# First half of a down projection as seven half-size block products in place of eight, on one Trainium2 core

## The chip, the core and the metric

The kernel runs on one core of one Trainium2 chip, in one launch. The metric is the device time of that core in microseconds. A time is the median of several executions. One further execution was recorded by the hardware profiler; the profile and the trace quoted below are from it.

The engines are TensorE (PE: matmuls; its weight loads are listed as PEld), VectorE (DVE), ScalarE (ACT), GpSimd (POOL) and SyncE (SP, which here issues most DMAs). Each works through its own queue in order and waits for the others on semaphores. PE writes into PSUM, which has eight banks of 512 float32 columns by 128 partitions; ACT and DVE read it, POOL does not in this kernel.

## The reference, cut to what matters

One encoder block over 512 tokens of width 1024. After the token mixers comes the feed-forward part, the only one that the change touches:

```python
def conv_glu_ffn(h, w_up, w_conv, b_conv, w_down):
    a, u = jnp.split(h @ w_up, 2, axis=-1)          # 2 x 2816 features
    return (jax.nn.gelu(dwconv3(a, w_conv, b_conv)) * u) @ w_down
...
x = x + merged @ w_out
x = x + conv_glu_ffn(rms_norm(x, ffn_norm_g), w_ffn_up, w_ffn_conv, b_ffn_conv, w_ffn_down)
return rms_norm(x, final_norm_g)
```

`w_down` is 2816 x 1024: 22 feature tiles of 128 by 8 output tiles of 128. All is float32.

## The kernel before

**Every product is three.** A float32 operand is split into a high part (rounded by a copy into the type float32r) and a low part (the difference). `mm3` (lines 212 to 215) multiplies high by high, high by low and low by high into one PSUM region. So a weight tile of 128 x 128 against 512 tokens is three matmuls of 512 columns, on lines 213, 214 and 215.

**The weights come in blocks.** `block_list` (line 63) names them in the order of use; each is up to 1024 columns by 128 partitions (512 KB), contiguous in `wflat`. `weights(key)` (line 201) is called where PE needs a block. It first issues the DMAs of blocks up to three ahead (`emit_raw`, into three buffers `wr`) and emits the splits of blocks up to one ahead (`emit_split`): ACT copies 512 columns into `wh` (line 195), DVE subtracts into `wl` (line 196), twice a block. `wh` and `wl` have four buffers each, that is, two blocks. A raw buffer comes free when its splits are done, a split buffer when PE has done its last matmul with it.

**The feed-forward loop** (lines 1289 to 1339) runs over two halves, `hh`, of eleven feature tiles each. For each feature tile `f` it projects `ua` and `uu` (24 matmuls of 512 columns each, into a bank of the pool `mm`), and between them runs a chain over the first: DVE scales by the row norm (line 456), ACT and DVE do the three-tap convolution (458 to 460), ACT and DVE the gelu (1315 to 1318), POOL multiplies by the row norm (1319). Then DVE multiplies with the second projection (1322) and ACT and DVE split the result into `UH[j]`, `UL[j]` (219, 220).

After eleven feature tiles comes the half's down projection: for each output tile, 11 x 3 matmuls of 512 columns accumulate into one bank, and DVE adds the bank to the residual `x2[f]` (line 1329). In the second half, output tiles 0 to 4 are done so; `last_tiles` does tiles 5 to 7: tile 5 in two halves of 256 tokens, tiles 6 and 7 for the first 256 tokens with the weights stationary, and for the last two groups of 128 tokens with the activations stationary and 256 weight columns moving (`dnl` blocks).

**What sets the order.** The source gives each engine's work in program order, and the framework's scheduler then reorders it within the dependences, so that splits of weights stand between the steps of the gate chain. Buffers that rotate (`wr`, `wh`, `wl`, the seven scratch tiles `scr`, the PSUM pools `mm` and `at` of four banks each) decide how far an engine may run ahead. The large activations lie in 15 `unit` buffers of 2112 float32 columns, four tiles of 512 and a margin of 64.

Of the kernel before, what the change touches and what calls it, by code (L numbers as in the profile page):

```python
# [17 lines left out]
P = 128  # L18
S = 512
# [3 lines left out]
M = 256  # L23
DFF = 2816
FT = DFF // P
HF = FT // 2
LF = KT - 2
NU = 15
WARM = 14
# [33 lines left out]
def block_list():  # L63

    L = []
    for i in range(4):
        L.append((("mlq", i), 1024))
    for f in range(4):
        L.append((("mlk", f), 1024))
    for c in range(3):  # L70
        for h in range(8 // TMK[c]):
            L.append((("tm", c, h), TMK[c] * TMC[c]))
    for n in ("xaq", "o", "memk", "memv", "naq", "nak"):
        for f in range(4):
# [8 lines left out]
    for hh in range(2):  # L83
        for f in range(HF * hh, HF * (hh + 1)):
            L.append((("ua", f), 1024))
            L.append((("uu", f), 1024))
        for f in range(8 if hh == 0 else LF):
            if hh == 1 and f >= LF - 3:
                i = f - LF + 3
                L.append((("dnl", i), 256 * (4 if i < 2 else 3)))  # L90
            for i, n in ((0, 8), (1, 3)):
                L.append((("dn", hh, f, i), n * 128))
    return L


# [15 lines left out]
def hybrid_block(ctx, tc, xg, xT, memT, wflat, vecs, gbias, nabias, outa, outb, outc):  # L111
# [18 lines left out]
    def unit(dt=F32):  # L130
        return up.tile([P, UNIT], dt, tag="unit", name=nm("u"))
# [11 lines left out]
        return atp.tile([P, 512], F32, tag="at", name=nm("at"))  # L143


    raws, split = {}, {}
    RAW_AHEAD, SPLIT_AHEAD = 3, 1
    st = {"raw": 0, "split": 0}

    def emit_raw(i):  # L150
        key, n = BLOCKS[i]
# [17 lines left out]
    def lastw(k, m):  # L169
# [3 lines left out]
        q = slice(k % 8 * 256, k % 8 * 256 + m)  # L173
        return lw[k // 8][:, HI256:][:, q], lw[2 + k // 8][:, q]

    def emit_split(i):
        key, n = BLOCKS[i]
        r = raws.pop(i)
        c, hs = halves(i)
        split[i] = []  # L180
        for a, b in hs:
            m = (b - a) * c
            if key[0] == "dnl":
                h, l = lastw(4 * key[1] + a, m)
            else:
                h = wp.tile([P, HWT], F32R, tag="hi", name=nm("wh"), bufs=4)
                l = wp.tile([P, HWT], F32R, tag="lo", name=nm("wl"), bufs=4)
                if key[:2] == ("tm", 2):
                    h = h[:, HI256:]
            for u, v in ((0, P), (P, 2 * P), (2 * P, m)) if i == 0 and a == 0 else ((0, m),):  # L190
                src = r[:, a * c + u:a * c + v]
                if i == 0 and u == 0:
                    st["wh1"] = V.tensor_copy(h[:, u:v], src).ins
                else:
                    A.activation(h[:, u:v], src, AF.Copy)  # L195
                V.tensor_tensor(l[:, u:v], src, h[:, u:v].bitcast(F32), op=ALU.subtract)  # L196
            for k in range(a, b):
                q = slice((k - a) * c, (k - a + 1) * c)
                split[i].append((h[:, q], l[:, q]))

    def weights(key):

        i, _, n = BINDEX[key]
        while st["raw"] <= min(i + RAW_AHEAD, len(BLOCKS) - 1):
            emit_raw(st["raw"])
            st["raw"] += 1
        while st["split"] <= min(i + SPLIT_AHEAD, len(BLOCKS) - 1):
            emit_split(st["split"])
            st["split"] += 1
        return split.pop(i)  # L210
# [948 lines left out]
    def last_tiles(U, UL_):  # L1159
# [63 lines left out]
        for t in range(2, NT):  # L1223
# [62 lines left out]
            V.scalar_tensor_tensor(o[:, LF * P:D], r, col, gfin, op0=ALU.mult, op1=ALU.mult)  # L1286
            SY.dma_start(outc[:, LF * P:], o[:, LF * P:D])

    for hh in range(2):
        gu = [unit(F32R) for _ in range(6)]  # L1290
        UH = [gu[k // 4][:, (k % 4) * S:(k % 4 + 1) * S] for k in range(HF)]
        UL = [gu[3 + k // 4][:, (k % 4) * S:(k % 4 + 1) * S] for k in range(HF)]
        for j in range(HF):
            f = HF * hh + j
# [23 lines left out]
            V.scalar_tensor_tensor(c, sq, 1.0, c, op0=ALU.add, op1=ALU.mult)  # L1318
            G.tensor_tensor(c, c, rb2, op=ALU.mult)  # L1319
# [3 lines left out]
            split_act(UH[j], UL[j], c, 0.5)  # L1323
        for f in range(KT if hh == 0 else LF - 1):
            ws = weights(("dn", hh, f, 0)) + weights(("dn", hh, f, 1))
            ps = mmps()
            for k in range(HF):
                mm3(ps, ws[k][0], ws[k][1], UH[k], UL[k], k == 0, k == HF - 1)
            V.tensor_tensor(x2[f], ps, x2[f], op=ALU.add)
            if hh == 1:  # L1330
                if f == 0:
                    A.activation(acc3, x2[f], AF.Square)
                else:
                    sq = scr()
                    A.activation(sq, x2[f], AF.Square)
                    G.tensor_tensor(acc3, acc3, sq, op=ALU.add)
                A.activation(x2[f], x2[f], AF.Copy, scale=vcol("fin_g", f))
        if hh == 1:
            last_tiles(UH, UL)


def _tiles(a):
# [4 lines left out]
def _layout(inp):  # L1347
# [14 lines left out]
    for key, n in BLOCKS:  # L1362
        kind = key[0]
        if kind == "mlq":
            b = wi[:, 2 * key[1]:2 * key[1] + 2, c_q:c_q + 512]
        elif kind in ("mlk", "o", "xaq", "naq", "nak"):
            c = {"mlk": c_k, "o": c_o, "xaq": c_xq, "naq": c_nq, "nak": c_nk}[kind] + key[1] * P
            b = wi[:, :, c:c + P]
        elif kind == "tm":
            _, c, h = key  # L1370
            ks = slice(TMK[c] * h, TMK[c] * (h + 1))
            if c == 0:
                b = np.concatenate([wi[:, ks, c_g:c_g + 16], wi[:, ks, c_v:c_v + 256]], axis=2)
            elif c == 1:
                b = np.concatenate([wi[:, ks, c_v + 256:c_v + 512], wi[:, ks, c_nv:c_nv + 256]], axis=2)
            else:
                b = wi[:, ks, c_nv + 256:c_nv + 512]
        elif kind == "memk":
            b = mkv[:, :, key[1] * P:(key[1] + 1) * P]
        elif kind == "memv":  # L1380
            b = mkv[:, 2 * key[1]:2 * key[1] + 2, 512:1024]
        elif kind == "g":
            gi = (0, 2, 1)[key[1]]
            c = c_m + gi * 1024 + key[2] * P
            b = wi[:, :, c:c + P]
        elif kind == "br":
            b = br[key[1]][:, :, key[2] * 256:(key[2] + 1) * 256]
        elif kind == "out":
            b = wo[:, :, key[1] * P:(key[1] + 1) * P]
        elif kind == "ua":  # L1390
            b = wu[:, :, key[1] * P:(key[1] + 1) * P]
        elif kind == "uu":
            b = wu[:, :, DFF + key[1] * P:DFF + (key[1] + 1) * P]
        elif kind == "dnl":
            k = HF + 4 * key[1]
            b = wd[:, k:k + n // 256, LF * P:]
        else:
            _, hh, f, i = key
            b = wd[:, HF * hh + 8 * i:HF * hh + 8 * i + n // P, f * P:(f + 1) * P]
# [54 lines left out]
```

## Time and profile before

| | us |
|---|---|
| median of 3 executions | 879.65 |
| lowest, highest | 879.35, 879.66 |
| span of the profiled execution, first to last instruction | 878.1 |
| PE busy in it | 872.7 |
| POOL busy in it | 127.1 |

Only the span is known of the profiled execution; its own time was not listed beside it. The granted TensorE clock was 0.999 over the span.

How to read the rows that follow: a row of a group gives source line, engine, operation, output<-inputs, shapes, count, then busy time and the mean ns of one, then the engine's idle time before such instructions and who ended it. A row of the timeline gives the start in us from the span's start, the duration, the engine, line, operation, operands and shape, and in brackets the idle time before it. A row of the windows gives for one stretch the busy time of each engine with its count of instructions, the granted clock, the DMA engines' share and GB/s.

### The profile page before, as it was taken

How to read it: one execution, taken by the hardware profiler on the slowest of the kernel's cores; microseconds unless marked ns; L12 is line 12 of the kernel's file. 1: busy time of each engine (PE TensorE's matmuls, PEld its weight loads, DVE VectorE, ACT ScalarE, POOL GpSimd, SP SyncE). 2: the span in 40 equal slices, each digit the busy share in tenths (PEclk: the TensorE clock that was granted, in tenths of full speed). 3: DMA queues.
4: the chain of work that ended last, by engine and by line, in shares of the span. 5: the costliest groups of instructions: out<-in, count | busy, mean ns of one | idle time of the engine just before them, and what ended most of it. 6: DMA issues, size and time to landing. Idle time of an engine off the chain costs nothing.

```text
span 878.1 us, 12238 instructions
## 1 busy us (share of the span) xinstructions
PE 872.7 (99%) x4334; PEld 740.4 (84%) x4334; DVE 582.2 (66%) x1211; ACT 451.4 (51%) x953; POOL 127.1 (14%) x203
## 2 busy tenths in 40 slices
PE   9999999999999999999999999999999999999997
PEld 7898889888888888888888888888888888888897
DVE  7694686775667758898676558776633466666433
ACT  7363555754456658888544435444422344444532
POOL 0101100001072460700000002111100011111011
PEclk9999999999999999999999999999999999999999
DMA  8224643522242354533223432222233322222412
GB/s 280 99 73 140 207 135 97 192 85 90 74 137 87 107 146 131 156 110 130 97 97 109 144 107 94 99 97 96 72 103 101 109 97 97 98 97 87 141 34 96
DMA packets 39421, 99.81 MB, mean 114 GB/s; under 512 B 5688, under 2 KB 13880, under 8 KB 39360
## 3 DMA queue, kind: packets, MB, share of 16 engines
q1 hardware_dynamic: 31568, 92.32, 31.1%
q0 software_dynamic: 7360, 6.32, 3.1%
q8 instruction: 34, 0.56, 0.3%
q10 hardware_dynamic: 432, 0.39, 0.1%
q14 instruction: 27, 0.22, 0.1%
HBM read 94.80 MB, written 4.21 MB: 113 GB/s over the span
## 4 chain that ended last, share of the span: by engine, by line
PE 99%; issue 0%; ACT 0%; DVE 0%; POOLq 0%; POOL 0%; DVEq 0%
PE mm L213 29%; PE mm L215 29%; PE mm L214 29%; PE at L214 2%; PE at L213 2%; PE at L215 2%; PE at L872 1%; PE at L725 1%; PE at L853 1%; PE at L727 1%; PE at L690 1%; PE at L834 0%; PE at L835 0%; PE at L706 0%; PE at L960 0%
## 5 line engine op out<-in xcount | busy, mean ns | idle before, releaser
L213 PE MATMUL mm<-u,wh 128*128 128x512 f32 (+1 forms) x1072 | 415.6, 388 | 0.0
L215 PE MATMUL mm<-u,wl 128*128 128x512 f32 (+1 forms) x1072 | 412.2, 385 | 0.0
L214 PE MATMUL mm<-u,wh 128*128 128x512 f32 (+1 forms) x1072 | 411.8, 384 | 0.0
L195 ACT ACTIVATE wh<-wr 128x512 fp32r<-128x512 f32 (+2 forms) x298 | 184.1, 622 | 234.4 <-PE mm L214 188.1
L196 DVE TENSOR_TENSOR wl<-wr,wh 128x512 fp32r<-128x512 f32 (+3 forms) x300 | 203.1, 678 | 92.4 <-ACT wh L195 85.8
L215 PEld LDWEIGHTS mm<-u,wl 128*128 128x128 f32 x1072 | 201.5, 188 | 40.1
L214 PEld LDWEIGHTS mm<-u,wh 128*128 128x128 f32 x1072 | 201.8, 188 | 38.8
L213 PEld LDWEIGHTS mm<-u,wh 128*128 128x128 f32 x1072 | 201.8, 188 | 38.2
L1319 POOL TENSOR_TENSOR s<-s,rb 128x512 f32<-128x512 f32 x22 | 38.3, 1739 | 250.0 <-DVE s L1318 238.1
L538 POOL DMA_DIRECT2D u<-nav_d x128 | 62.2, 512 | 66.5 <-PE at L872 22.5
L219 ACT ACTIVATE u<-s 128x512 fp32r<-128x512 f32 x26 | 16.4, 630 | 57.5 <-DVE s L1322 56.1
L1322 DVE TENSOR_TENSOR s<-mm,s 128x512 f32<-128x512 f32 x22 | 15.2, 691 | 25.1 <-POOL s L1319 25.1
L458 ACT ACTIVATE s<-pad,vec 128x512 f32<-128x512 f32 x30 | 24.4, 813 | 9.5 <-DVE pad L456 9.5
L459 DVE SCALAR_TENSOR_TENSOR s<-pad,vec,s 128x512 f32<-128x512 f32 x30 | 23.6, 786 | 6.1 <-ACT s L458 6.0
L220 DVE SCALAR_TENSOR_TENSOR u<-s,u 128x512 fp32r<-128x512 f32 x26 | 18.0, 691 | 14.1 <-ACT u L219 14.0
L1318 DVE SCALAR_TENSOR_TENSOR s<-s,s 128x512 f32<-128x512 f32 x22 | 15.2, 692 | 13.4 <-ACT s L1317 13.3
L317 POOL TENSOR_TENSOR rc<-y,nhalf 128x4 f32<-128x4 f32 x1 | 1.0, 1032 | 152.9 <-DVE y L314 152.9
L460 DVE SCALAR_TENSOR_TENSOR s<-pad,vec,s 128x512 f32<-128x512 f32 x30 | 22.5, 750 | 0.7
L1317 ACT ACTIVATE s<-s 128x512 f32<-128x512 f32 x22 | 13.9, 632 | 15.1 <-DVE s L1316 15.1
L456 DVE TENSOR_TENSOR pad<-mm,rb 128x512 f32<-128x512 f32 x22 | 15.1, 691 | 7.3 <-PE mm L215 6.5
L213 PE MATMUL mm<-wh,u 128*128 128x512 f32 x48 | 18.9, 394 | 0.0
L214 PE MATMUL mm<-wl,u 128*128 128x512 f32 x48 | 18.8, 392 | 0.0
(315 smaller groups left out, 1028.4 us busy)
## 6 DMA issues: line engine op xcount, KB each, us to landing
wr<-wflat SPq DMA_DIRECT2D x141, 512.0 KB, 3.3
nab<-nabias SPq DMA_DIRECT2D x16, 256.0 KB, 2.7
u<-nav_d POOLq DMA_DIRECT2D x128, 32.0 KB, 2.6
s<-xT SPq DMA_DIRECT2D x15, 256.0 KB, 3.9
wr<-wflat SPq DMA_DIRECT2D x14, 192.0 KB, 2.3
nav_d<-nv POOLq DMA_DIRECT2D x8, 256.0 KB, 2.4
R<-rd SPq DMA_DIRECT2D x8, 256.0 KB, 3.9
wr<-wflat SPq DMA_DIRECT2D x2, 544.0 KB, 3.3
```

Of the source, the lines that this page charges most:

```text
L195: A.activation(h[:, u:v], src, AF.Copy)
L196: V.tensor_tensor(l[:, u:v], src, h[:, u:v].bitcast(F32), op=ALU.subtract)
L213: PE.matmul(ps, lh, rh, start=start, stop=False)
L214: PE.matmul(ps, lh, rl, start=False, stop=False)
L215: st["mm"] = PE.matmul(ps, ll, rh, start=False, stop=stop).ins
L219: A.activation(h, src, AF.Copy, scale=scale)
L220: V.scalar_tensor_tensor(l, src, scale, h.bitcast(F32), op0=ALU.mult, op1=ALU.subtract)
L458: A.activation(t1, pad[:, 0:512], AF.Identity, scale=vcol(w, i), bias=vcol(b, i))
L459: V.scalar_tensor_tensor(t1, pad[:, 1:513], vcol(w, n + i), t1, op0=ALU.mult, op1=ALU.add)
L460: V.scalar_tensor_tensor(t1, pad[:, 2:514], vcol(w, 2 * n + i), t1, op0=ALU.mult, op1=ALU.add)
L538: G.dma_start(vw[r * 32:(r + 1) * 32, i * 256:(i + 1) * 256], nav_v[hf, r, CW[b]:CW[b] + 32, hp * 256:(hp + 1) * 256])
L1319: G.tensor_tensor(c, c, rb2, op=ALU.mult)
```

## The change

The first half shrinks from eleven feature tiles to ten, the second grows to twelve. For the first half, two feature tiles, two output tiles and two halves of the tokens form a product of 2 x 2 blocks. The blocks are 128 x 128 of the weights and 128 x 256 of the activations. It is computed in Winograd's form of Strassen's scheme: seven products of 256 columns instead of eight, with four sums of weight blocks and four sums of activation blocks formed first, and the seven results combined afterwards. Each of the seven products is again three matmuls (`mm3`), and accumulates in PSUM over the five feature pairs.

- `emit_sum`: POOL forms the weight sums from the raw block, three additions, up to two blocks ahead. A new block kind `ds` carries two feature pairs (1024 columns) or one (512) of one output pair, three blocks for each of the four output pairs.
- `split_block`: ACT and DVE split seven weight tiles per feature pair instead of four. The sums' parts go to tiles `sh`, `sl`, with four buffers each.
- `strip`: after every second feature tile DVE forms the activation sums (four operations of 256 columns), and ACT and DVE split 7 x 256 columns instead of 4 x 256 (two tiles). The strips are placed 16 or 48 float32 past the start of a `unit`.
- `products`: 105 matmuls of 256 columns per output pair into four banks, from `at` and `mm` in turn. Then one ACT copy, three DVE operations of 256 columns and two of 512 that read PSUM, and two POOL additions of 512 close the pair.

```diff
-HF = FT // 2
+HFS = (10, 12)
+HF = HFS[1]
+NP = HFS[0] // 2
...
+    for fp in range(4):
+        for b in range((NP + 1) // 2):
+            L.append((("ds", fp, b), 512 * min(2, NP - 2 * b)))
...
-    RAW_AHEAD, SPLIT_AHEAD = 3, 1
+    RAW_AHEAD, SUM_AHEAD, SPLIT_AHEAD = 3, 2, 1
...
+    def emit_sum(i):
...
+        r, w = raws[i], n // 4
+        s31 = tp.tile([P, S], F32, tag="E", name=nm("s31"))[:, :2 * w]
+        s24 = tp.tile([P, S], F32, tag="nab", name=nm("s24"))[:, :2 * w]
+        G.tensor_tensor(s31, r[:, :2 * w], r[:, w:3 * w], op=ALU.add)
+        G.tensor_tensor(s24[:, :w], s31[:, w:], r[:, :w], op=ALU.add)
+        G.tensor_tensor(s24[:, w:], s24[:, :w], r[:, 3 * w:4 * w], op=ALU.add)
...
+    def split_block(i):
...
+        for src, names, small in ((r[:, :w], ("a11",), True), (r[:, 2 * w:4 * w], ("a22", "a12"), True),
+                                  (s31, ("s3", "s1"), False), (s24, ("s2", "s4"), False)):
...
+                h = tp.tile([P, S], F32R, tag="R", name=nm("sh"), bufs=4)[:, :m]
+                l = tp.tile([P, S], F32R, tag="H", name=nm("sl"), bufs=4)[:, :m]
+            A.activation(h, src, AF.Copy)
+            V.tensor_tensor(l, src, h.bitcast(F32), op=ALU.subtract)
...
+    def products(fp):
+
+        bank = [(mmps if fp % 2 else atps)() for _ in range(4)]
...
+        (p2, p3), (p4, p5), (p1, p6) = [halves_of(t) for t in bank[:3]]
+        p7 = bank[3][:, :S // 2]
+        plan = (("a11", p1, "b11", True, False), ("a12", p2, "b21", True, False), ("s4", p3, "b22", False, True),
+                ("a22", p4, "t4", True, False), ("s1", p5, "t1", False, True), ("s2", p6, "t2", False, True),
+                ("s3", p7, "t3", True, True))
+        for p in range(NP):
+            g = p % 2
+            if g == 0:
+                ws = weights(("ds", fp, p // 2))
+            gs = slice(g * P, (g + 1) * P)
+            for a, ps, b, first, last in plan:
+                (wh, wl), (xh, xl) = ws[a], strips[p][b]
+                mm3(ps, wh[:, gs], wl[:, gs], xh, xl, first and p == 0, last and p == NP - 1)
...
+        A.activation(z[:, :Hs], p1, AF.Copy)
+        V.tensor_tensor(u[:, :Hs], p6, z[:, :Hs], op=ALU.subtract)
+        V.scalar_tensor_tensor(z[:, Hs:], u[:, :Hs], -1.0, p5, op0=ALU.mult, op1=ALU.subtract)
+        V.tensor_tensor(u[:, Hs:], u[:, :Hs], p7, op=ALU.add)
+        V.tensor_tensor(r1, bank[0], r1, op=ALU.add)
+        V.tensor_tensor(r2, bank[1], r2, op=ALU.add)
+        G.tensor_tensor(r1, r1, z, op=ALU.add)
+        r2v = r2.rearrange("p (a b) -> p a b", a=2)
+        G.tensor_tensor(r2v, r2v, u[:, Hs:].unsqueeze(1).to_broadcast([P, 2, Hs]), op=ALU.add)
...
+    def strip(c):
...
+        b1, b2 = held.pop(), c
+        p, Hs = len(strips), S // 2
+        sh = 16 if p < 3 else 48
...
+        V.tensor_tensor(t13[:, lo], b1[:, hi], b1[:, lo], op=ALU.subtract)
+        V.tensor_tensor(t24[:, lo], b2[:, hi], t13[:, lo], op=ALU.subtract)
+        V.tensor_tensor(t13[:, hi], b1[:, hi], b2[:, hi], op=ALU.subtract)
+        V.tensor_tensor(t24[:, hi], b2[:, lo], t24[:, lo], op=ALU.subtract)
...
+        for src, names in ((b1[:, lo], ("b11",)), (b2, ("b21", "b22")), (t13, ("t1", "t3")), (t24, ("t2", "t4"))):
+            h, l = place(Hs * len(names))
+            split_act(h, l, src, 0.5)
...
-        for f in range(KT if hh == 0 else LF - 1):
+        if hh == 0:
+            for fp in range(4):
+                products(fp)
+            continue
+        for f in range(LF - 1):
```

In the changed program the addition of a pair's first bank to the residual is on line 1358, that of its second on line 1359; the closing POOL additions are on 1360 and 1362, the splits of the new blocks on 209 and 210, the weight sums on 190 to 192.

More of the change, by code (lines that the diff above doesn't have):

```diff
@@ L82, in block_list @@
         L.append((("out", f), 1024))
[L83 to L92, printed above, removed]
+    for f in range(HFS[0]):
+        L.append((("ua", f), 1024))
+        L.append((("uu", f), 1024))
+    for fp in range(4):
+        for b in range((NP + 1) // 2):
+            L.append((("ds", fp, b), 512 * min(2, NP - 2 * b)))
+    for f in range(HFS[0], FT):
+        L.append((("ua", f), 1024))
+        L.append((("uu", f), 1024))
+    for f in range(LF):
+        if f >= LF - 3:
+            L.append((("dnl", f - LF + 3), 1024))
+        for i, n in ((0, 8), (1, 4)):
+            L.append((("dn", 1, f, i), n * 128))
     return L
@@ L143, in atps @@
         return atp.tile([P, 512], F32, tag="at", name=nm("at"))
-    raws, split = {}, {}
-    RAW_AHEAD, SPLIT_AHEAD = 3, 1
-    st = {"raw": 0, "split": 0}
+    raws, split, sums = {}, {}, {}
+    RAW_AHEAD, SUM_AHEAD, SPLIT_AHEAD = 3, 2, 1
+    st = {"raw": 0, "sum": 0, "split": 0}
     def emit_raw(i):
@@ L206, in weights @@
             st["raw"] += 1
+        while st["sum"] <= min(i + SUM_AHEAD, len(BLOCKS) - 1):
+            emit_sum(st["sum"])
+            st["sum"] += 1
         while st["split"] <= min(i + SPLIT_AHEAD, len(BLOCKS) - 1):
@@ L1398, in _layout @@
             _, hh, f, i = key
-            b = wd[:, HF * hh + 8 * i:HF * hh + 8 * i + n // P, f * P:(f + 1) * P]
+            b = wd[:, HFS[0] + 8 * i:HFS[0] + 8 * i + n // P, f * P:(f + 1) * P]
         b = np.ascontiguousarray(b).reshape(P, -1)
```

86 lines of the change are left out of this document (69 added, 17 removed).

## The prediction

> **What bounds the kernel now.** I read the page's first lines first, then the chain of work that ended last, then the groups by line, then the timeline of TensorE and the windows in the feed-forward part.
>
> ```profile
> span 878.1 us, 12238 instructions
> PE 872.7 (99%) x4334; PEld 740.4 (84%) x4334; DVE 582.2 (66%) x1211; ACT 451.4 (51%) x953; POOL 127.1 (14%) x203
> ...
> PE 99%; issue 0%; ACT 0%; DVE 0%; POOLq 0%; POOL 0%; DVEq 0%
> ```
>
> TensorE (PE) is the whole chain, so the span moves by what is taken out of the row of matmuls, plus each time that row has to wait. The window inside the first down projection shows what the other engines do there now:
>
> ```profile
> core 0: us, PE busy (x) PEld busy (x) DVE busy (x) ACT busy (x) POOL busy (x), PEclk, DMA share, GB/s
> 632.00:691.80 59.80, 59.80 (x265) 49.52 (x264) 21.77 (x34) 14.95 (x25) 0.28 (x1) 1.00 0.30 99
> ```
>
> The stage runs at the full granted clock (1.00), VectorE (DVE) is busy 21.8 of 59.8 us and GpSimd (POOL) 0.3. That cover is what the change spends.
>
> A matmul's "mean ns" (384 to 388 on the page) is not its price, since the records overlap. The price is the distance from start to start:
>
> ```profile
> 799.75 0.39 PE L213 MATMUL mm<-u,wh 128*128 128x512 f32 x1
> ...
> 843.95 0.39 PE L213 MATMUL mm<-u,wh 128*128 128x512 f32 x1
> ...
> 846.67 0.28 PE L213 MATMUL mm<-u,wh 128*128 128x256 f32 x1
> ...
> 850.63 0.28 PE L213 MATMUL mm<-u,u 128*128 128x256 f32 x1
> ...
> 858.28 0.28 PE L215 MATMUL mm<-u,u 128*128 128x256 f32 x1
> ```
>
> ```profile
> 83.52 0.28 PE L213 MATMUL at<-wh,u 128*128 128x256 f32 x1
> ...
> 94.71 0.28 PE L215 MATMUL at<-wh,u 128*128 128x256 f32 x1
> ```
>
> - 512 columns: 195 steps (65 triples) in 44.20 us, 0.2267 us each.
> - 256 columns, both operands at addresses that are multiples of 256 bytes: 33 steps to 850.63 in 3.96 us, 0.1200 each.
> - 256 columns, one operand 192 bytes off such an address: 65 steps in 7.65 us, 0.1177; and 95 steps in 11.19 us, 0.1178.
>
> Half the columns thus cost 52 to 53% of a full matmul, so seven halves for eight must give 12.5% and pay back about 4%.
>
> **The change on TensorE.** The first half has now 8 output tiles x 11 feature tiles x 3 = 264 matmuls of 512 columns: 264 x 0.2267 = 59.84 us (the window above lies inside it). Afterwards: 4 output pairs x 5 feature pairs x 7 products x 3 = 420 matmuls of 256. The new strips lie 64 or 192 bytes off (`sh`), the weights on multiples of 256, so I take 0.1177: 49.43 us; the other bound, 0.1200, gives 50.40. The eleventh feature tile moves to the second half and costs there 5 x 3 full matmuls (3.40), 6 of 256 columns for the tile done in two halves (0.72), and 12 more in the last tiles (1.41): 5.53 us. Sum: 49.43 + 5.53 - 59.84 = **-4.88 us**, at 0.1200 **-3.91**. The weight load does not forbid it: loads of 0.19 us follow each other 0.12 apart while 256-column matmuls run.
>
> ```profile
> 850.51 0.19 PEld L213 LDWEIGHTS mm<-u,u 128*128 128x128 f32 x1
> 850.63 0.19 PEld L214 LDWEIGHTS mm<-u,u 128*128 128x128 f32 x1
> ```
>
> **Handovers on PSUM.** An output pair now takes four banks, alternating between the two pools. The order lists of the built program put the addition that frees the first bank (L1358 there) ahead of the rest; that bank's products p2 and p3 are finished four products before the pair ends, 12 x 0.1177 = 1.4 us, and the addition takes 0.69 us (row below). So the next up projection, which needs this bank, should not wait; if the addition came last it would cost about 2 us, once.
>
> ```profile
> L1329 DVE TENSOR_TENSOR u<-mm,u 128x512 f32<-128x512 f32 x13 | 9.0, 692 | 14.6 <-PE mm L215 14.6
> ```
>
> **What the weights now need.** An output pair takes PE 105 x 0.1177 = 12.36 us. For it come three raw blocks (two feature pairs, two, one). POOL makes sums of each (adds of 512, 256, 256 columns; 256, 128, 128 for the small one), ACT and DVE split 1792 columns instead of 1024, and each pair ends with five DVE operations that read PSUM and two POOL additions of 512. Rows:
>
> ```profile
> L195 ACT ACTIVATE wh<-wr 128x512 fp32r<-128x512 f32 x278 | 173.4, 628 | 210.3 <-PE mm L214 168.0 <-PE mm L215 10.5 <-DMA wr<-wflat 9.1
> L1177 ACT ACTIVATE s<-u 128x256 f32<-128x256 f32 x4 | 1.7, 416 | 8.1 <-DVE u L1175 8.1
> L196 DVE TENSOR_TENSOR wl<-wr,wh 128x512 fp32r<-128x512 f32 x279 | 191.4, 687 | 75.6 <-ACT wh L195 69.0 <-PE at L214 2.0 <-PE at L310 2.0
> L717 DVE TENSOR_TENSOR E<-E,u 128x256 f32<-128x256 f32 x8 | 3.3, 418 | 0.4 <-ACT E L714 0.4
> L717 DVE TENSOR_TENSOR E<-E,u 128x128 f32<-128x128 f32 x8 | 2.2, 280 | 0.0
> L1336 POOL TENSOR_TENSOR acc<-acc,s 128x512 f32<-128x512 f32 x4 | 5.2, 1295 | 32.7 <-ACT s L1335 32.7
> L584 POOL MEMSET s<- 100x512 f32 x1 | 0.5, 536 | 0.4 <-PE mm L214 0.4
> L283 POOL MEMSET msk<- 128x128 f32 x2 | 0.4, 204 | 0.0
> ```
>
> ACT: two blocks of 0.42 + 3 x 0.63 and one of about 1.6 make 6.2 us of 12.36; not a bound. No row has a 256-wide addition on POOL: it lies between half of 1.295 (0.65) and all of it. The two MEMSETs (a quarter of the columns, 38% of the time) say that POOL's time falls with the columns apart from some 0.1 us, so 0.75 for 256 and 0.45 for 128. POOL per pair: 2 x (1.29 + 2 x 0.75) + 0.75 + 2 x 0.45 + 2 x 1.29 = 9.8 us. DVE's splits: 2 x (0.42 + 3 x 0.69) + 0.28 + 3 x 0.42 = 6.5 us. Each fits alone. Together they don't, if they exclude each other, and the trace says they do:
>
> ```profile
> 532.90 0.75 DVE L459 SCALAR_TENSOR_TENSOR s<-pad,vec,s 128x512 f32<-128x512 f32 x1
> ...
> 540.32 0.69 DVE L196 TENSOR_TENSOR wl<-wr,wh 128x512 fp32r<-128x512 f32 x1
> ...
> 540.92 1.78 DVE L459 SCALAR_TENSOR_TENSOR s<-pad,vec,s 128x512 f32<-128x512 f32 x1
> ...
> 619.57 0.69 DVE L196 TENSOR_TENSOR wl<-wr,wh 128x512 fp32r<-128x512 f32 x1
> ```
>
> ```profile
> 540.54 1.62 POOL L1319 TENSOR_TENSOR s<-s,rb 128x512 f32<-128x512 f32 x1 [3.86 <-PE mm L215]
> ...
> 547.25 1.29 POOL L1319 TENSOR_TENSOR s<-s,rb 128x512 f32<-128x512 f32 x1 [5.09 <-DVE s L1318]
> ...
> 619.61 1.80 POOL L1319 TENSOR_TENSOR s<-s,rb 128x512 f32<-128x512 f32 x1 [9.08 <-DVE s L1318]
> ```
>
> POOL alone takes 1.29; started 0.04 us into a DVE split it takes 1.80, that is, its 1.29 begin 0.55 us after the split began. L459, issued while POOL ran, took 1.78 in place of 0.75: POOL's record ended at 542.16, L459's at 542.70, so it began in effect 0.2 us before POOL's record ended. From start to start a split holds the other off 0.55 us and a POOL addition 1.09, in turns. The Trainium skill has this as a rule (SBUF — State Buffer, "Who interferes with whom"): a VectorE instruction with two SBUF inputs and a GpSimd instruction that reads SBUF block each other wholly, and one with a single SBUF input doesn't. By that rule the PSUM-reading additions are free of it; the rows above agree on the blocking.
>
> By holds (256 wide: 0.28 and 0.55; 128: 0.15 and 0.28) a pair asks 4.85 (DVE) + 7.7 (POOL) = 12.5 us against PE's 12.36: just balanced, so what counts is deadlines. I walked the order lists for the second pair, t = 0 where PE starts on it. After the splits of its second block have freed the sum buffers, at t = 4.0 (the first closing additions, three splits and the small block's sums come first), the queues are, on DVE: one split of 512; 128, 256, 256, 256 (the small block); 256, 512, 512, 512 (next pair's first block): 3.5 us. On POOL: additions of 512; 512, 512 (the closing additions of the pair before); 256, 256; then 512, 256, 256: 6.6 us. In turns they end at 14.2, and 14.4 with the split's own 0.14 of tail. PE's third product of the third pair wants this last split's result at 12.36 + 8 x 0.1177 = 13.3. **Loss 1.1 us**, and the same at the fourth pair. At the second pair POOL isn't yet behind: raw blocks arrive late,
>
> ```profile
> wr<-wflat SPq DMA_DIRECT2D x141, 512.0 KB, 3.3
> ```
>
> so its closing additions fall later. For the first pair the tight place is the last feature pair: the tenth gate product on POOL stands behind the sums of a block whose load can only be issued 1.4 us into that up projection, 3.3 us before it lands. By the same walk the strips and the small block's splits end 16.0 us after that projection's partner started, and are wanted at 16.3: I add 0.3 us for all such near misses. DMA bytes are unchanged. Strips, formed by four more DVE operations per pair in the up stage, lie under 37 us of matmuls per pair and cost nothing unless the chain above slips.
>
> Sum: -4.88 + 2 x 1.1 + 0.3 = -2.4 us. The profiled execution's span is 878.1, the median of the runs 879.65, that is 1.55 us around it, which the change doesn't touch: span 875.7, time **877.3 us**.
>
> **Rivals.**
> 1. *No wait at all.* The turns hide everything, since POOL's sums run a pair ahead: 879.65 - 4.88 = 874.8. For it: a balance of 12.5 to 12.36 is within the error of my holds. Against: the deadline comes 1 us too early at two places.
> 2. *Slower: DVE and POOL in turns set the pace.* Place: the first block of the third and fourth output pairs. Price: if the full records count (no overlap at the hand-over), DVE's nine take 4.72 and POOL's eight 4 x 1.29 + 4 x 0.75 = 8.16, and the start of this stretch slips to about 4.9; the end is 17.8, the loss 4.5 at each: -4.88 + 9.0 = +4.1, 883.8. It decides for slower from 2.4 us per place. For it: eight additions that have never run densely beside splits. Against: the 540 us rows, where the hand-over overlaps.
> 3. *No change.* PE at 0.1200 (strip offsets don't help) and 2.5 us of waits: -3.91 + 2.5 = -1.4, 878.2; or 4.9 us of waits, 879.65.
> 4. *The change doesn't do what it says*, half-size products bound by weight loads of 0.19: 420 x 0.188 = 79 us, 909. The PEld rows exclude it (chance under 1%, left out).
>
> **How the numbers follow.** Forecast (waits of 1 to 3.1 us) 0.42; rival 1 0.15; rival 3 0.17; rival 2 0.26. 0.2% of 879.65, about what measurement tells from no change, is 1.76 us. Faster: 0.42 + 0.15 = 0.57; within: 0.17; slower: 0.26. Range: from rival 1 to rival 2, 874.6 to 884.0; the forecast's own is 876 to 878.
>
> **What would show it.** Right: 420 matmuls of 256 columns at 0.1177 wherever they run unbroken; gaps of about 1 us before the second and third products of output pairs three and four, released by DVE's low parts (the new split lines); POOL's additions at 1.6 to 1.8 us rather than 1.29 in that stage. Rival 1: no gap over 0.3 us. Rival 2: gaps of 4 us there. Wrong: gaps that ACT, a DMA or a PSUM bank releases, a wait at the next up projection, or a half matmul at over 0.121.

## The result, and the profile after

| | before | after |
|---|---|---|
| median, us | 879.51 | 887.6 |
| lowest, highest, us | 879.35, 879.66 | 886.92, 887.68 |
| span of the profiled execution, us | 878.1 | 885.3 |

The ratio is 1.009, 95% interval 1.0075 to 1.0104: the kernel became slower by 8 us. The forecast was 2.4 us faster, and the time lies above the forecast's range (884.0).

The page of the changed kernel, its first lines and the shares of the chain of waits:

```profile
span 885.3 us, 12834 instructions
...
PE 872.4 (99%) x4523; PEld 747.0 (84%) x4523; DVE 625.4 (71%) x1277; ACT 465.9 (53%) x991; POOL 176.0 (20%) x247
...
PE 94%; DVE 3%; issue 1%; DMA 1%; POOL 1%; ACT 1%; SPq 0%; POOLq 0%; DVEq 0%
```

PE was 99% of the chain and is 94%: the rest of the span hangs on DVE, POOL, a DMA and ACT. PE's busy time hides the change (872.7 and 872.4), in part because matmuls that run slower, as some do here, count in full. So TensorE's start-to-start distances are read, as in the prediction. Its timeline in the new stage (`mm3` is on lines 258 to 260 there; edits move it by some lines in the runs below):

```profile
618.88 0.39 PE L258 MATMUL at<-u,wh 128*128 128x256 f32 x1
619.10 0.28 PE L259 MATMUL at<-u,wh 128*128 128x256 f32 x1
621.39 0.55 PE L260 MATMUL at<-u,wl 128*128 128x256 f32 x1 [2.00 <-DVE wl L210]
...
622.09 0.41 PE L259 MATMUL at<-u,wh 128*128 128x256 f32 x1
623.18 0.58 PE L260 MATMUL at<-u,wl 128*128 128x256 f32 x1 [0.68 <-DVE wl L210]
623.56 0.41 PE L258 MATMUL at<-u,sh 128*128 128x256 f32 x1
...
628.25 0.30 PE L259 MATMUL at<-u,sh 128*128 128x256 f32 x1
...
644.59 0.28 PE L258 MATMUL mm<-u,wh 128*128 128x256 f32 x1
...
651.78 0.28 PE L259 MATMUL at<-u,sh 128*128 128x256 f32 x1
654.00 0.39 PE L260 MATMUL at<-u,sl 128*128 128x256 f32 x1 [1.94 <-DVE sl L210]
...
666.55 0.28 PE L259 MATMUL mm<-u,sh 128*128 128x256 f32 x1
667.97 0.39 PE L260 MATMUL mm<-u,sl 128*128 128x256 f32 x1 [1.14 <-DVE sl L210]
...
679.50 0.28 PE L260 MATMUL mm<-u,sl 128*128 128x256 f32 x1
679.69 0.47 PE L258 MATMUL mm<-u,wh 128*128 128x512 f32 x1
```

- From the first product (618.88) to the next up projection (679.69) the stage takes **60.81 us**. At 0.1177 us for each of its 420 matmuls it would take 49.43: 11.38 are lost.
- First pair, first products: six steps from 618.88 to 623.56 take 4.68 us, where 0.71 would do: **3.97** lost, to the low parts of a11 and then a12.
- From 623.56 to 628.25, 22 steps take 4.69 us, 0.213 each: **2.10** lost, without any wait.
- Third and fourth pair, third product: 2.22 and 1.42 us for one step: **2.10** and **1.30** lost.
- The rest, about 1.9 us, is in small waits, 1.0 of it in the first pair's last feature pair.
- From 644.59 to 651.78 nothing waits: 61 steps in 7.19 us, 0.1178 each. And the step into the next up projection is 0.19 us: no bank is late.

The 22 slow steps have their reason in the granted clock. Windows of the changed kernel (columns as in the prediction):

```profile
618.90:636.20 17.30, 14.17 (x90) 13.40 (x91) 14.33 (x24) 7.42 (x16) 7.07 (x8) 0.80 0.21 61
...
621.40:628.20 6.80, 6.12 (x26) 5.76 (x27) 5.75 (x9) 3.16 (x6) 2.06 (x3) 0.50 0.27 77
...
646.00:660.00 14.00, 12.06 (x101) 11.72 (x100) 14.00 (x17) 6.20 (x13) 13.61 (x12) 1.00 0.33 95
```

From 621.40 to 628.20, right behind the 2 us wait, TensorE was granted half its clock (0.50). The last row shows the second cost: between 646 and 660 us both DVE (14.00) and POOL (13.61 of 14) are never idle, while PE has 1.9 us of holes. The groups by shape between 600 and 690 us say why:

```profile
L190 POOL TENSOR_TENSOR s<-wr 128x512 f32<-128x512 f32 x8 | 14.0, 1755 | 16.4 <-DMA wr<-wflat 11.8 <-DVE sl L210 4.6
L192 POOL TENSOR_TENSOR s<-s,wr 128x256 f32<-128x256 f32 x8 | 8.0, 999 | 0.6
...
L190 POOL TENSOR_TENSOR s<-wr 128x256 f32<-128x256 f32 x4 | 4.0, 1003 | 1.4 <-DMA wr<-wflat 0.8 <-DVE sl L210 0.6
...
L210 DVE TENSOR_TENSOR wl<-wr,wh 128x256 fp32r<-128x256 f32 x12 | 9.6, 802 | 0.0
L210 DVE TENSOR_TENSOR wl<-wr,wh 128x512 fp32r<-128x512 f32 x8 | 8.4, 1054 | 0.0
```

Beside each other a split of 512 takes 1.05 us for 0.69, one of 256 0.80 for 0.42, a POOL addition of 512 1.76 for 1.29, one of 256 1.00. Alone, POOL's additions are close to what the prediction took (0.72, 0.52 and 1.28 in the rows below, for 0.75, 0.45 and 1.29), and one row shows that the two engines do not take turns. From the timeline of DVE and POOL:

```profile
618.55 1.53 DVE L210 TENSOR_TENSOR sl<-s,sh 128x512 fp32r<-128x512 f32 x1
...
637.43 1.29 DVE L210 TENSOR_TENSOR sl<-s,sh 128x512 fp32r<-128x512 f32 x2
638.63 0.68 DVE L1358 TENSOR_TENSOR u<-at,u 128x512 f32<-128x512 f32 x1
```

```profile
617.81 1.72 POOL L1435 TENSOR_TENSOR s<-s,rb 128x512 f32<-128x512 f32 x1
620.33 0.72 POOL L190 TENSOR_TENSOR s<-wr 128x256 f32<-128x256 f32 x1 [0.80 <-DMA wr<-wflat]
621.13 0.52 POOL L191 TENSOR_TENSOR s<-s,wr 128x128 f32<-128x128 f32 x1
...
626.87 1.28 POOL L190 TENSOR_TENSOR s<-wr 128x512 f32<-128x512 f32 x1 [4.62 <-DMA wr<-wflat]
...
636.32 3.55 POOL L190 TENSOR_TENSOR s<-wr 128x512 f32<-128x512 f32 x1 [4.62 <-DVE sl L210]
```

The addition that started at 636.32 took 3.55 us. DVE's splits followed each other without a gap until 638.7; then DVE read PSUM (L1358), and POOL ended at 639.87, that is 1.2 us later, about its time alone. It had waited for several splits in a row, not for one. The Trainium skill (SBUF — State Buffer, "Who interferes with whom") calls the ports that the two engines share an exclusive lock, and says of VectorE's modes with two ports that whoever issues first has them for the whole instruction and the other blocks fully. The blocking agrees with the row of 3.55 us. Who comes next after an instruction the page does not say, and here it was DVE again.

Last, the chain of waits into the first products, in order of time (start, us, what):

```profile
610.52 3.46 DMA wr<-wflat
...
614.04 1.53 POOL s L190
...
615.64 1.08 POOL s L191
...
616.79 1.07 POOL s L192
...
617.88 0.64 ACT sh L209
...
618.55 1.08 DVE sl L210
...
620.01 0.68 DVE s L1438
620.68 0.65 DVE wl L210
```

The load of the second block (0,1) could only be issued at 610.5, when a raw buffer came free, and landed at 614.0. POOL then made that block's three sums, and only after them the gate product of the ninth feature tile (L1435, 617.81 to 619.53), which was in its queue behind them. DVE needs that product at L1438. Ahead of L1438 in DVE's own queue stands the split of the second block's last sums, which had waited for the third sum; it was issued at 618.55, ran beside the gate product and ended at 620.08, so that it and not the product ended last. Behind L1438 stands the split of a11, with which PE begins. By either way the sums of a block that PE needs 42 matmuls (4.9 us) later held up the block that it needed at once.

### The profile page after: what moved, and what is told of

It reads as the page before. It is cut to its first block, busy times and chain, and to the rows that moved or that the text cites. A ratio compares the mean times of both kernels' runs of the same rounds, so it can differ in the third digit from the quotient of the medians.

```text
span 885.3 us, 12834 instructions
## 1 busy us (share of the span) xinstructions
PE 872.4 (99%) x4523; PEld 747.0 (84%) x4523; DVE 625.4 (71%) x1277; ACT 465.9 (53%) x991; POOL 176.0 (20%) x247
## 4 chain that ended last, share of the span: by engine, by line
PE 94%; DVE 3%; issue 1%; DMA 1%; POOL 1%; ACT 1%; SPq 0%; POOLq 0%; DVEq 0%
PE mm L258 26%; PE mm L260 26%; PE mm L259 26%; PE at L260 3%; PE at L259 3%; PE at L258 3%; PE at L917 1%; PE at L770 1%; DMA wr<-wflat 1%; PE at L898 1%; PE at L772 1%; PE at L735 1%; DVE wl L210 1%; DVE sl L210 1%; DVE u L265 1%
## 5 line engine op out<-in xcount | busy, mean ns | idle before, releaser
L258 PE MATMUL mm<-u,wh 128*128 128x512 f32 (+1 forms) x1021 | 392.2, 384 | 0.2 <-ACT wh L237 0.2
L260 PE MATMUL mm<-u,wl 128*128 128x512 f32 (+1 forms) x1021 | 389.0, 381 | 0.0
L259 PE MATMUL mm<-u,wh 128*128 128x512 f32 (+1 forms) x1021 | 388.2, 380 | 0.0
L237 ACT ACTIVATE wh<-wr 128x512 fp32r<-128x512 f32 (+1 forms) x274 | 170.8, 627 | 185.3 <-PE mm L259 149.8
L238 DVE TENSOR_TENSOR wl<-wr,wh 128x512 fp32r<-128x512 f32 (+2 forms) x276 | 189.5, 689 | 64.6 <-ACT wh L237 57.4
L260 PEld LDWEIGHTS mm<-u,wl 128*128 128x128 f32 x1021 | 191.9, 188 | 37.9 <-DVE wl L238 1.0
L258 PEld LDWEIGHTS mm<-u,wh 128*128 128x128 f32 x1021 | 192.0, 188 | 35.4 <-ACT wh L237 0.6
L259 PEld LDWEIGHTS mm<-u,wh 128*128 128x128 f32 x1021 | 192.1, 188 | 35.2
L1435 POOL TENSOR_TENSOR s<-s,rb 128x512 f32<-128x512 f32 x22 | 36.9, 1675 | 175.4 <-DVE s L1434 171.5
L264 ACT ACTIVATE u<-s 128x512 fp32r<-128x512 f32 (+1 forms) x36 | 21.1, 600 | 59.4 <-DVE s L1438 57.6
L1438 DVE TENSOR_TENSOR s<-mm,s 128x512 f32<-128x512 f32 x22 | 15.2, 691 | 26.1 <-POOL s L1435 26.1
L265 DVE SCALAR_TENSOR_TENSOR u<-s,u 128x512 fp32r<-128x512 f32 (+1 forms) x36 | 24.8, 704 | 10.1 <-ACT u L264 10.1
L503 ACT ACTIVATE s<-pad,vec 128x512 f32<-128x512 f32 x30 | 24.4, 813 | 10.2 <-DVE pad L501 10.2
L1434 DVE SCALAR_TENSOR_TENSOR s<-s,s 128x512 f32<-128x512 f32 x22 | 16.7, 760 | 12.1 <-ACT s L1433 11.9
L190 POOL TENSOR_TENSOR s<-wr 128x512 f32<-128x512 f32 (+1 forms) x12 | 18.1, 1504 | 17.8 <-DMA wr<-wflat 12.6
L210 DVE TENSOR_TENSOR sl<-s,sh 128x512 fp32r<-128x512 f32 (+1 forms) x24 | 21.4, 916 | 0.1
```

Of the source, the lines that this page charges most:

```text
L210: V.tensor_tensor(l, src, h.bitcast(F32), op=ALU.subtract)
L258: PE.matmul(ps, lh, rh, start=start, stop=False)
L259: PE.matmul(ps, lh, rl, start=False, stop=False)
L260: st["mm"] = PE.matmul(ps, ll, rh, start=False, stop=stop).ins
L265: V.scalar_tensor_tensor(l, src, scale, h.bitcast(F32), op0=ALU.mult, op1=ALU.subtract)
L503: A.activation(t1, pad[:, 0:512], AF.Identity, scale=vcol(w, i), bias=vcol(b, i))
```

## The experiments

"Stage" is the time from the first product's matmul to the next up projection, read from each trace's timeline of TensorE as above; plain products take 54.40 us for the same part (second experiment). "Half clock" is the time at a granted clock of 0.50 in or right ahead of the stage, "POOL" its busy time between 618.9 and 690.6 us. In e4_warm 2.17 us of matmuls on constants stand ahead of the stage. The ratio is to the kernel before, which took 879.3 us in these runs.

| run | us | ratio, 95% interval | stage | POOL | half clock |
|---|---|---|---|---|---|
| the change | 887.6 | 1.009, 1.0075 to 1.0104 | 60.81 | 44.6 | 6.8 |
| e1_nosum | 876.5 | 0.9967, 0.9956 to 0.9979 | 50.55 | 14.8 | 0 |
| e7_uneven | 879.14 | 0.9997, 0.9987 to 1.0006 | 54.40 | 3.6 | 0 |
| e2_order | 885.68 | 1.0073, 1.0058 to 1.0088 | 60.12 | 43.3 | 3.4 |
| e3_gate_dve | 886.02 | 1.0079, 1.0063 to 1.0096 | 59.13 | 43.6 | 3.4 |
| e4_warm | 887.21 | 1.009, 1.0075 to 1.0105 | 58.51 | 45.2 | 3.4 |
| e5_sums_unused | 888.35 | 1.0102, 1.0087 to 1.0117 | 59.00 | 43.9 | 10.2 |
| e6_sums_dve | 882.01 | 1.0034, 1.0021 to 1.0047 | 56.99 | 14.6 | 0 |
| e8_close_dve | 886.47 | 1.0081, 1.0066 to 1.0096 | 60.62 | 34.4 | 6.8 |
| e9_wide_pool | 885.44 | 1.0072, 1.0057 to 1.0087 | 59.82 | 25.2 | 3.4 |
| e10_narrow_pool | 884.51 | 1.0058, 1.0043 to 1.0073 | 58.13 | 33.8 | 0 |
| e11_sums_late | 880.67 | 1.0019, 1.001 to 1.0028 | 55.26 | 14.6 | 0 |
| e12_nosum_offset0 | 877.11 | 0.9974, 0.9963 to 0.9984 | 51.73 | 14.8 | 0 |
| e13_late_gate | 879.54 | 1.0001, 0.9992 to 1.001 | 53.37 | 13.2 | 0 |
| e14_late_gate_swap | 880.51 | 1.0012, 1.0003 to 1.0022 | 54.94 | 13.2 | 0 |

**No weight sums.** Everything else of the change stays.

```diff
-        G.tensor_tensor(s31, r[:, :2 * w], r[:, w:3 * w], op=ALU.add)
-        G.tensor_tensor(s24[:, :w], s31[:, w:], r[:, :w], op=ALU.add)
-        G.tensor_tensor(s24[:, w:], s24[:, :w], r[:, 3 * w:4 * w], op=ALU.add)
+        s31, s24 = r[:, :2 * w], r[:, 2 * w:4 * w]
```

> Leaves out the three POOL additions of each weight block; the splits read raw slices in their place, so the splits, the matmuls and the closing work keep their number and size and only the sums' values are missing. Theory A (POOL's sums hold DVE's splits off and stand in front of the gate product): nearly all waits of the down projection go, 12 us of them, and the time is 876 to 878 us. Theory B (ACT's and DVE's splits of 1792 columns a block are too many by themselves): the waits at the third and fourth output pair stay, 883 us or more.

876.5 us. TensorE's timeline:

```profile
618.60 0.28 PE L254 MATMUL at<-u,wh 128*128 128x256 f32 x1
...
631.07 0.28 PE L254 MATMUL at<-u,wh 128*128 128x256 f32 x1
...
668.89 0.28 PE L256 MATMUL mm<-u,sl 128*128 128x256 f32 x1
669.15 0.47 PE L254 MATMUL mm<-u,wh 128*128 128x512 f32 x1
```

Its window:

```profile
618.90:690.60 71.70, 71.24 (x514) 66.57 (x514) 55.48 (x98) 34.98 (x70) 14.83 (x10) 1.00 0.36 114
```

The stage takes 50.55 us, 1.1 more than 49.43, and from 631.07 to 668.89 nothing waits. Seven products, the strips, 75% more weight splits and the closing operations are all hidden; the 11 us hang on 36 POOL additions. What they take from DVE can be read directly: in this window 43 splits of the new blocks keep DVE busy 26.8 us, and in the change 45 of them 40.5 us.

**Uneven halves alone**: the kernel before with halves of 10 and 12 feature tiles and plain products.

```diff
-HF = FT // 2
+HFS = (10, 12)
+HF = HFS[1]
...
-            for i, n in ((0, 8), (1, 3)):
+            for i, n in ((0, 8), (1, HFS[hh] - 8)):
```

> One part alone: the kernel before with halves of 10 and 12 feature tiles and plain products. All theories: one feature tile of 24 matmuls of 512 columns (5.44 us) turns into 15 of 512 and 18 of 256 (5.53 us): +0.1 us against the kernel before, same within 0.2%.

879.14 us, no difference. TensorE's first matmul of the first down projection, and that of the next up projection:

```profile
618.32 0.39 PE L214 MATMUL mm<-u,wh 128*128 128x512 f32 x1
...
672.72 0.39 PE L214 MATMUL mm<-u,wh 128*128 128x512 f32 x1
```

240 matmuls in 54.40 us, 0.2267 each. This is what the changed stage is to be held against: 54.40 to 60.81 is the loss of 6.4, 54.40 to 50.55 the gain without sums.

**Are the sums late, or in the way?** Two runs mend the order that the chain showed: POOL takes the gate products of the last two feature tiles ahead of later blocks' sums and DVE the first block's splits ahead of the second's (e2_order), or DVE takes these two gate products itself (e3_gate_dve). A third lets POOL form all sums, but nobody reads them (e5_sums_unused).

```diff
+        with ExitStack() as es:
+            if key[1:] in ((0, 1), (0, 2), (1, 0)):
+                es.enter_context(tc.issue_after(st["gate", 8 if key[1:] == (0, 1) else 9]))
...
+                if key == ("ds", 0, 1):
+                    for first in st["wl00"]:
+                        es.enter_context(tc.issue_after(first))
```

> All the work is kept; only queue order: POOL takes the gate products of feature tiles 8 and 9 ahead of the sums of the later blocks, and the splits of the second block's sums stand behind the splits of the first block's raw tiles. Theory A (the wait at the first output pair is a matter of order: a split that PE needs stands behind a gate product that stands behind sums whose load is late): the 4.0 us of waits there, the 0.6 us before it and the 2.1 us at half clock go, about 881 us. Theory B (the port shared by DVE and POOL is simply full there): the wait moves but stays, 886 to 888 us.

```diff
-            G.tensor_tensor(c, c, rb2, op=ALU.mult)
+            (V if f in (8, 9) else G).tensor_tensor(c, c, rb2, op=ALU.mult)
```

> The gate products of feature tiles 8 and 9 move from POOL to DVE; nothing else. Theory A: DVE no longer waits for POOL ahead of the first block's splits, 881 to 882 us. Theory B (port full): 886 us or more.

```diff
         G.tensor_tensor(s24[:, w:], s24[:, :w], r[:, 3 * w:4 * w], op=ALU.add)
+        s31, s24 = r[:, :2 * w], r[:, 2 * w:4 * w]
```

> POOL makes all weight sums as before, but the splits read raw slices in their place, so nothing waits for the sums' values; the output lacks the sums. POOL's load, and what it holds of the port, is the whole of it. Theory A (the splits wait for late sums): as without the sums, 876 to 878 us. Theory B (POOL's additions hold DVE off, whoever needs their result): 883 to 887 us.

The first two gave 885.68 and 886.02: 1.6 to 1.9 us, not the 4 of the first wait, and at or near the figures of the theory that the port is full. In e2_order the wait at the first products shrank to 1.6 us, and a wait of 3.0 us appeared at the first pair's last feature pair, at 631.8:

```profile
634.90 0.58 PE L269 MATMUL at<-u,wl 128*128 128x256 f32 x1 [2.86 <-DVE wl L217]
```

The third gave 888.35, as slow as the change itself and 1.4 us above the range of its slower theory, though no split waited for a sum: PE's stage took 59.00 us and it had lost another 3 us ahead of it. Against e1_nosum, which differs from it by POOL's additions alone, that is 11.9 us; about 4.2 of it are slow steps at half clock. One thing that POOL makes was still waited for, the gate products, which stand in its queue behind the sums (waits between 600 and 690 us: sum, times, longest):

```profile
DVE s L1439 <- POOL s L1436: 3.1, 2, 1.9
```

e3_gate_dve takes the last two of these products off POOL's queue and gains 1.6 us of 11. So most of the cost is POOL working beside DVE's splits (and holding the raw blocks that it reads until it is done; the two were not separated), less of it the late gate products, and an order that mends one wait moves it to the next.

**Who adds.** All weight sums on DVE (e6_sums_dve); the closing additions on DVE (e8_close_dve); the sums shared both ways (e9_wide_pool, e10_narrow_pool). In that order, G becomes V on lines 190 to 192, on 1360 and 1362, on 191 and 192, and on 190 alone.

> The weight sums move from POOL to DVE, the closing additions stay on POOL. DVE then has per output pair 5.6 (splits) + 2.4 (PSUM) + 3.4 (sums) us from start to start, 11.4 of 12.4, plus two holds of 1.1. Theory A (the alternation with POOL is what costs): 880 to 883 us. Theory B (the sum of work is too much for whichever engine): 886 us or more.

> The two closing additions of each output pair move from POOL to DVE. Theory A (they crowd the port just where the next pair's first block is split): the waits at the third and fourth pair, 2.2 and 1.4 us, fall under 1 us each, 885 to 886 us. Theory B (sums, not closing additions): no change or slower, 887.5 to 889 us.

> The wide addition of a block's sums (512 or 256 columns, L190) stays on POOL, the two narrow ones (L191, L192) go to DVE. POOL's holds on the shared port per output pair fall from 7.7 us (5.5 of them sums) to about 4.9, DVE's work rises by 2.0 us. Theory A (the loss is POOL's time on the port, nearly in proportion): half way between 887.6 (all sums on POOL) and 882.0 (all on DVE), 884 to 885.5. Theory B (with all sums on DVE the DVE queue itself is the bound, so that the work is best shared): below 881.5.

> The other half: the wide addition (L190) on DVE, the two narrow ones on POOL, which takes them about 1.0 us each in this stage for 256 columns. POOL keeps 16 narrow additions of 256 and 8 of 128 columns. Theory A: 884 to 885.5, or 1 us more if each start of a POOL instruction costs the port a fixed time besides its columns. Theory B: below 881.5.

All sums on DVE gave 882.01, 5.6 us under the change, though DVE got 36 instructions more. Its window:

```profile
618.90:690.60 71.70, 66.80 (x486) 62.33 (x486) 62.75 (x123) 32.09 (x65) 14.58 (x10) 1.00 0.34 107
```

DVE is busy 62.75 us with 123 instructions; in the change it is busy 63.49 with 91 over the same window:

```profile
618.90:690.60 71.70, 65.37 (x468) 61.67 (x469) 63.49 (x91) 31.64 (x64) 44.61 (x40) 0.95 0.32 100
```

So the time of the 32 added instructions is less than what DVE stood blocked while POOL made the same sums. The two mixes lie between (885.44 and 884.51, both inside the 884 to 885.5 of the theory that blames POOL's time on the port), but not in proportion to POOL's time: with the wide additions alone on POOL it is busy 25.2 us and the stage takes 1.7 us longer than with the narrow ones and 33.8. Some 1.2 of these 1.7 are slow steps at half clock, and the intervals of the two times overlap, so the two mixes can't be ranked. With the closing additions on DVE the time was 886.47, between its two theories: the waits of the third and fourth pair were gone, and a new one of 2.8 us stood at the second pair, with another stretch of half clock.

**The half clock.** 20 matmuls on constants keep TensorE busy ahead of the first product.

```diff
+        if fp == 0:
+            with tc.issue_after(st["mm"]):
+                for _ in range(20):
+                    last = PE.matmul(bank[3][:, S // 2:], one[:, :P], one, start=True, stop=True).ins
```

> Twenty matmuls of 256 columns on constants into an unused half bank, ahead of the first product, where PE waits 2.2 us anyhow. Theory A (the 22 matmuls at 0.213 us that follow the wait run at half the granted clock because PE stood idle): the half clock goes, 2 us less than the changed kernel, 885.5 us. Theory B (they are slow because of their operands or of other engines' traffic): no change, 887.6 us, or up to 2 us more.

887.21, near the 887.6 of the second theory and not the 885.5 of the first. Yet the first theory has the cause right: the half clock at the first pair was gone, but it came at the third:

```profile
651.54 0.28 PE L259 MATMUL at<-u,sh 128*128 128x256 f32 x1
653.75 0.39 PE L260 MATMUL at<-u,sl 128*128 128x256 f32 x1 [1.93 <-DVE sl L210]
```

```profile
650.90:654.30 3.40, 1.47 (x12) 1.27 (x12) 3.40 (x4) 1.80 (x5) 3.24 (x4) 1.00 0.54 154
654.30:657.70 3.40, 3.40 (x18) 3.40 (x17) 3.40 (x7) 0.94 (x2) 3.24 (x4) 0.50 0.22 48
```

The half clock follows the waits: here, filled away at one place, it came at another. Which waits bring it, the last section works out.

**What is left with the sums on DVE.** In e6_sums_dve 6.5 of the stage's 7.6 us of waits lie in the first one and a half pairs. Late sums: a block's sums go right ahead of its splits (e11_sums_late). Then the last two gate products on DVE too (e13_late_gate), and the splits of s2, s4 ahead of those of s3, s1 (e14_late_gate_swap).

```diff
-    RAW_AHEAD, SUM_AHEAD, SPLIT_AHEAD = 3, 2, 1
+    RAW_AHEAD, SUM_AHEAD, SPLIT_AHEAD = 3, 1, 1
...
-                                  (s31, ("s3", "s1"), False), (s24, ("s2", "s4"), False)):
+                                  (s24, ("s2", "s4"), False), (s31, ("s3", "s1"), False)):
```

> All sums on DVE as in the earlier run (882.0), but those of a block are put right ahead of its splits and not one block earlier (SUM_AHEAD 1 for 2), so that no sums of a later block stand in DVE's order before the splits of the first. Theory A (the waits left there, 1.8 us at the start of the first pair and 2.0 in its last feature pair, are DVE's order): 879 to 880.5. Theory B (they are DVE's total work, 13 us per pair against PE's 12.4): 882 +- 1, the waits only move.

> As the run with late sums on DVE (880.7), and the gate products of the last two features (L1435, feature tiles 8 and 9) on DVE too, so that POOL has no instruction at all between the strips and the first closing addition. There DVE waited 1.2 us for POOL's gate product right before the first pair's splits, and 1.0 us of a narrow sum was held off by the second. Theory A (POOL's presence beside DVE's splits is the cost at the first pair as well): the 5.3 us of waits of the first one and a half pairs fall by 1.5 to 2.5, 878.2 to 879.2, level with the kernel before or under it. Theory B (DVE's own load is the bound there, 13 us per pair, and grows by 1.4): 880.5 to 882.

> The run e13_late_gate with one more edit: a block's second sums (s2, s4) are split ahead of its first (s3, s1), since TensorE uses s4 as third product and s1 as fifth. Theory A (the wait of 0.7 us in the first pair's last feature pair is the order of these two): 0.5 to 1 us under e13_late_gate. Theory B (it is DVE's total work): the same as e13_late_gate within 0.4.

880.67, 879.54 and 880.51. The first missed its 879 to 880.5 by 0.2 and gained 1.3 us; the second took another 1.1 and lies 0.3 over its forecast; the third lost 1.0 where 0.5 to 1 was to be gained, with a wait of 2.0 us back at the first products, so the order of the two splits was not what was missing. e13_late_gate is level with the kernel before (1.0001). Its window:

```profile
618.90:690.60 71.70, 69.76 (x502) 64.88 (x501) 64.20 (x127) 33.74 (x68) 13.17 (x9) 1.00 0.33 107
```

The stage is 53.37 us, 1.0 under plain products and 3.9 over its matmuls, with DVE busy 64.2 of 71.7 us. Of the runs that form the sums and use them, none is faster than the kernel before.

**Where the strips lie.** e1_nosum with the strips on multiples of 256 bytes.

```diff
-        sh = 16 if p < 3 else 48
+        sh = 0
```

> As the run without weight sums (876.5; the splits of the sums read the raw block), but the strips lie at addresses that are multiples of 256 bytes (sh = 0 for 16 and 48). Theory A (the start-to-start distance of a 256-column matmul depends on where its columns lie): 0.1200 for 0.1177 us at 420 matmuls, +1.0 us, 877.5. Theory B (it does not, and the 0.1200 seen elsewhere has another cause): 876.5 +- 0.3.

```profile
630.97 0.28 PE L254 MATMUL at<-u,wh 128*128 128x256 f32 x1
...
670.07 0.28 PE L256 MATMUL mm<-u,sl 128*128 128x256 f32 x1
```

The same stretch without waits takes 39.10 us here and 37.82 in e1_nosum (631.07 to 668.89): 1.3 us more in the stretch (326 steps of 0.1199 for 0.1160), 1.2 in the stage. In the times it is 0.6 us (877.11 to 876.5), where the two intervals overlap, so that the time alone decides for neither theory and the trace does for the first. The offsets in the change do what the prediction took from them.

## Why the prediction was wrong, step by step

- **The matmul term, -4.88.** Right. 61 steps at 0.1178 in the change itself, 326 at 0.1160 in e1_nosum; in e1_nosum the stage came to 50.55 for 54.40, and e7_uneven shows that the move of a feature tile costs nothing. The weight load bounds nothing.
- **The handover on PSUM.** Right: 0.19 us for the step into the next up projection.
- **ACT is no bound, DMA bytes unchanged, strips hidden.** Right: e1_nosum keeps all of them and waits 1.1 us in all.
- **POOL's prices.** Right alone: 0.72 for the 0.75 taken, 1.28 for 1.29, 0.52 for 0.45; and in the stage 1.76 for a 512, as its signs said (1.6 to 1.8).
- **"In turns".** Here the sum began to fail. The hold times of 0.55 and 1.09 came from single meetings of a POOL and a DVE instruction. In a dense row DVE does not hand over after each split (3.55 us for one addition). So the two engines together, "just balanced" at 12.5 to 12.36 us, were over PE's time: DVE 14.00 and POOL 13.61 of 14 us with PE waiting.
- **1.1 us at the third and fourth pair.** Right in place, in the releaser (DVE's low parts) and in kind, too small: 2.1 and 1.3, 3.4 for 2.2. (The walk's own figures, 4.0, 3.5 and 6.6, add up to 14.1 and not 14.2; that 0.1 us explains nothing.)
- **"For the first pair the tight place is the last feature pair", 0.3 us.** This is the step that failed. The walk over the queues began at the second pair. At the first pair's first products, POOL's sums of the next block stand ahead of a gate product, and this product and the splits of those sums stand ahead of the first block's splits: 4.0 us, and 1.0 more at the last feature pair. On top, the wait brought 2.1 us of half clock, which the prediction had nowhere.
- **Rival 2**, DVE and POOL as the pace, is what happened. Its price of 4.5 us for a place was too high and its two places were too few: it said 883.8.

In sum: waits of 2.5 us were forecast and 11.4 came inside the stage. 60.81 - 54.40 = 6.4; PE starts the stage 0.6 us later than in e7_uneven (618.88 and 618.32), and 0.9 us more lies behind the kernel's last matmul (5.80 us from its start to the end of the span, 4.86 in e7_uneven; 5.1 to 5.3 in the other runs with the seven products), whose cause stays open.

## What to carry to other kernels

VectorE and GpSimd don't add up where both read two operands from SBUF: cost a GpSimd instruction there by what it takes from VectorE, and try it on VectorE first. Walk the queues from the first use of a new stage, where the last work of the stage before still stands in them, and not from its steady state. A forecast of waits on TensorE that add up to 2 us within some 3.4 should carry a further 1 to 3 us for the clock (here 1.1 to 1.6 for one stretch of 3.41 us, 2.1 and 2.6 for the two of 6.83).

## What was not expected of the hardware

Apart from the first and last microseconds of a run, TensorE's granted clock fell to 0.50 nine times: for 6.83 us in the change and once in e5_sums_unused, for 3.41 us in seven other places (e2, e3, e4, e5, e9, and twice in e8). Each time PE had just waited or was still waiting. All single waits of 2.4 us and more brought such a stretch. Of those around 2 us some did and some did not: in the change the 2.2 us at the first pair, but not the 2.1 at the third, while the 2.1 at the same place in e4_warm did.

The traces say what tells them apart. In every run each change of the granted clock lies a whole multiple of 3.413 us after the run's first one, to within 0.01 us: in the change it first rises at 3.65, falls at 621.46 (181 times 3.413 later) and rises at 628.29 (183 times). So time can be cut into windows of 3.413 us, and what PE lost in each added up (its start-to-start distances beyond 0.2267 or 0.1177). Of the windows at full clock:

| run | window from, us | PE lost in it, us | clock behind it |
|---|---|---|---|
| e8_close_dve | 644.2 | 2.78 | 0.50 |
| the change, first pair | 618.0 | 2.59 | 0.50 |
| e4_warm, third pair | 650.9 | 2.20 | 0.50 |
| e5_sums_unused | 616.4 | 2.09 | 0.50 |
| e10_narrow_pool | 618.2 | 2.01 | 1.00 |
| e3_gate_dve, third pair | 650.9 | 1.99 | 1.00 |
| the change, third pair | 652.2 | 1.93 | 1.00 |

The nine windows with 2.09 to 3.06 us lost were all followed by half clock, and none of the others, in any of the sixteen traces, with at most 2.01. So it is the sum within one window that counts, not the single wait: the 2.1 us at the third pair of the change began 0.3 us ahead of a window's edge, while those of e4_warm lay in one window, and in e3_gate_dve three waits of 1.4, 0.5 and 0.8 us together were enough (2.71). Where the bound lies is known only roughly, as what PE lost is an estimate: by the idle time of TensorE's records the change's third pair (1.82) and e5_sums_unused (1.76) change places.

The Trainium skill (TensorE: Matmul & The Clock Gate, "Part 1: The HAM clock gate") has a free-running window of 3413 ns, and half rate after a whole idle window. The window agrees; but here some three fifths of a window were enough.
